# Opening stage of a two-layer encoder trunk: where the position-bias lines, the modulation sums and the first weight split stand

## The chip, the cores and the metric

The kernel runs on one core of one Trainium2 chip. The metric is the device time of one execution in microseconds (us); lower is better. Five engines work side by side, each through its own list of instructions in order: TensorE (PE, matrix products, with PEld for its weight loads), VectorE (DVE), ScalarE (ACT), GpSimd (POOL) and SyncE (SP, which here only issues transfers). The profile also records the TensorE clock that was granted, as a share of full speed.

## The reference

Two layers act on x of 1024 tokens by 1024 features. Each layer first modulates its input with a vector computed from a condition c, then mixes tokens, then normalises:

```python
mod = jax.nn.silu(c) @ ada_w[i] + ada_b[i]
shift, scale, gate = jnp.split(mod[:, None, :], 3, axis=-1)
u = x * (1 + scale) + shift
y = mixer_dilated(u, a_w_in[j], a_w_out[j], rel_bias)      # layer 0
x = layernorm(DEEPNORM_ALPHA * x + gate * y, ln_g[i], ln_b[i])
```

Layer 0 projects u with `a_w_in` to q, k, v and a gate (1152 columns each) and runs windowed attention in 18 heads of three groups with dilations 1, 4 and 16. The logits get a bias that depends only on the distance between key and query: a row of a 32-row table per bucket of distance and head. Layer 1 is a latent attention; the change does not touch it. All data are float32.

## The kernel before, in words

A float32 product is made of three faster ones. Each operand is split into a rounded "high" part (`uh`, `wh`) and the rest (`ul`, `wl`); the product is wh.uh + wl.uh + wh.ul, summed in PSUM (`mm3`, L90). The split of a 128x1024 weight tile (`w_split`, L102) is one ScalarE pass for the high part and one subtraction, on VectorE in the opening, for the low part.

Features lie on partitions. The 1024 features of u are eight **channel blocks** dd = 0 to 7 of 128 features by 1024 tokens. The opening (`startup`, L156) forms u block by block as its data land, and projects it at once to the q, k and v columns of head pair 0: three weight blocks b = 0, 1, 2, each two PSUM banks of 512 tokens. A channel block gives each weight block six 512-column products (`in_block`, L254): three parts by two halves, so 18 in all and 144 for the opening. When they end, `layer_a_attention` (L657) begins the projections of the next pair (L92 to L94).

For each channel block, the shift and the scale of its 128 features are needed as a column, 256 sums over 1024 values of silu(c). The weights `ada` for that come in two tiles of 128 x 1024, one MB together; they hold eight chunks k of 256 columns. `mod_acc` (L206) adds up SHARE[dd] of the chunks on VectorE into one tile, each term a 128x256 instruction. `mod_sums` (L218) sums over partitions on TensorE: one matmul of one column for each chunk left and one for the VectorE tile, for shift and for scale. The profile shows each such float32 matmul as two rows. `mod_col` (L229) adds the bias column `bcol` on ScalarE, `u_hi` (L236) makes uh (and u itself, which replaces x in `xc`) on ScalarE, `u_lo` (L247) makes ul on VectorE.

While the first data travel, TensorE multiplies zeros (`zeros`, L163; ZEROS = (10, 6) gives the ten at the start and the six after the first sums, and one stands after every second matmul of the first sums).

The **position-bias lines** are one line of 512 values for each head: a 33-row one-hot table (`onehot`, 198 KB) multiplied with the bias table `rel_bias`, one matmul for each head group (`bias_line`, L336, L341 in the profile, two rows each), copied by ScalarE (L343), and written to DRAM (`bias_write`), from where `bias_tile` (L349) loads shifted copies. Before the change the tables are loaded on SP at channel block 2, line 0 is computed after block 5, and lines 1 and 2 stand at the head of `layer_a_attention`, which in the trace places them ahead of the last channel block.

In the opening every engine keeps the order in which the code is written (`manual_schedule`). In the layers behind it only TensorE and SP do; the order on ScalarE, VectorE and GpSimd is chosen there by a planner when the kernel is built. Loads of the opening go on SP's queue in written order; c and the bias columns go on ScalarE's. Large tiles come from a pool G of 33 buffers; PSUM has eight banks, six of which hold the accumulating products. `weave` (L49) interleaves lists of matmuls by their progress against a given total.

In step dd of the loop, the sums of block dd are done in one piece, then its column and u are made while the products of block dd - 1 run.

Of the kernel before, what the change touches and what calls it, by code (L numbers as in the profile page):

```python
# [15 lines left out]
F32 = mybir.dt.float32  # L16
F32R = mybir.dt.float32r
AF = mybir.ActivationFunctionType
# [51 lines left out]
class Trunk:  # L70
# [85 lines left out]
    def startup(self):  # L156
# [6 lines left out]
        def zeros(n):  # L163
            for _ in range(n):
                nc.tensor.matmul(pz, zt[:, 0:P], zt[:, P : P + 512], start=True, stop=True)

        zeros(ZEROS[0])
# [3 lines left out]
        nc.scalar.activation(self.sc, self.sc, AF.Silu)  # L171
        self.rb = KP.tile([33, P], F32, name="rb")
        nc.gpsimd.memset(self.rb, NEG)
        raws = {}
        adas, xcs = {}, {}

        def load_ada(dd):
            t = [self.gt(F32, "ada") for _ in range(2)]
            for j in range(2):
                sync.dma_start(t[j], A["ada_ss0"][dd, :, j * 1024 : (j + 1) * 1024])  # L180
            return t

        def load_x(dd):
            t = self.gt(F32, "xc")
            sync.dma_start(t, A["xt"][dd])
            return t

        def load_d(dd):
            adas[dd], xcs[dd] = load_ada(dd), load_x(dd)
# [6 lines left out]
        raws[2] = self.w_load(A["wa"][2])  # L196
# [6 lines left out]
        acc_psum = [[self.bank("ip") for _ in range(2)] for _ in range(3)]  # L203
        accs, pms = {}, {}

        def mod_acc(dd):  # L206
            w = [adas[dd][k // 4][:, (k % 4) * 256 : (k % 4) * 256 + 256] for k in range(8)]
            n = SHARE[dd]
            parts = [(w[k], self.sc[:, k : k + 1]) for k in range(8 - n)]
            if n:  # L210
                a = KP.tile([P, 256], F32, tag="ot", bufs=3, name=self.nm("acc"))
                nc.vector.tensor_scalar(a, w[8 - n], self.sc[:, 8 - n : 9 - n], None, op0=ALU.mult)
                for k in range(9 - n, 8):
                    nc.vector.scalar_tensor_tensor(a, w[k], self.sc[:, k : k + 1], a, op0=ALU.mult, op1=ALU.add)
                parts.append((a, self.ones))
            accs[dd] = parts

        def mod_sums(dd):  # L218

            parts = accs.pop(dd)  # L220
            pm = pms[dd] = self.bank("pm")
            for j in range(2):
                for i, (w, x) in enumerate(parts):
                    nc.tensor.matmul(
                        pm[:, j : j + 1], w[:, j * P : j * P + P], x, start=i == 0, stop=i == len(parts) - 1
                    )
                    yield 1.0

# [21 lines left out]
        def all_of(gen):  # L250
            for _ in gen:
                pass

        def in_block(dd, blocks=(0, 1, 2)):  # L254
            for b in blocks:
                h, l = whl[b]
                ks = slice(dd * P, dd * P + P)
                hh, hl, lh = (h, self.uh[dd]), (h, self.ul[dd]), (l, self.uh[dd])
                if dd or b:
                    todo = [(x, hf) for x in (hh, lh, hl) for hf in range(2)]  # L260
                else:
                    todo = [(hh, 0), (hl, 0), (hh, 1), (lh, 0), (lh, 1), (hl, 1)]
                seen = set()
                for n, ((w, u), hf) in enumerate(todo):
                    nc.tensor.matmul(  # L265
                        acc_psum[b][hf], w[:, ks], u[:, hf * 512 : hf * 512 + 512],
                        start=dd == 0 and hf not in seen, stop=dd == NK - 1 and n >= 4,
                    )
                    seen.add(hf)
                    yield 1.0  # L270
# [12 lines left out]
        u_lo(0, HALVES[0])  # L283
        split(0)
        u_hi(0, HALVES[1])
        u_lo(0, HALVES[1])
        all_of(in_block(0, (0,)))
        split(1)
        mod_acc(1)
        weave((in_block(0, (1,)), 6.0), (mod_sums(1), 12.0))  # L290
        split(2)
        for dd in range(1, NK):
            if dd + 2 < NK:
                load_d(dd + 2)
            if dd == 2:
                self.bias_load()
            if dd == NK - 2:
                self.a_prefetch(3)
            if dd > 1:
                all_of(mod_sums(dd))  # L300
# [5 lines left out]
            if dd == 4:  # L306
                self.bias_split()
            all_of(in_block(dd - 1, (2,) if dd == 1 else (0, 1, 2)))
            if dd == 6:
                self.bias_line(0)  # L310
        self.bias_write(0)
        all_of(in_block(NK - 1))
# [8 lines left out]
    def bias_load(self):  # L321


        nc, A = self.nc, self.A
        rb = self.rb
        rr = rb[0:32, 0:96].rearrange("a (g h) -> a g h", g=3)[:, :, 0:6]
        nc.sync.dma_start(rr, A["rel_bias"].rearrange("a (g h) -> a g h", g=3))
        oh = self.KP.tile([33, 3 * 512], F32, tag="vt", bufs=1, name="oh")
        nc.sync.dma_start(oh, A["onehot"])
        self.bias_in = rb, oh  # L330

    def bias_split(self):
# [3 lines left out]
    def bias_line(self, g):  # L336

        nc = self.nc
        rb, oh = self.bias_in
        pl = self.bank("pl")  # L340
        nc.tensor.matmul(pl, rb, oh[:, g * 512 : g * 512 + 512], start=True, stop=True)  # L341
        rows = slice(32 * g, 32 * g + 6)
        nc.scalar.copy(self.lines[rows, :], pl[rows, :])  # L343

    def bias_write(self, g):

        (self.nc.scalar if g else self.nc.sync).dma_start(self.lines_d[g], self.lines[32 * g : 32 * g + 6, :])

    def bias_tile(self, head):  # L349

# [306 lines left out]
    def layer_a_attention(self):  # L657
        nc = self.nc
        self.o = {}
        for g in (1, 2):  # L660
            self.bias_line(g)
            self.bias_write(g)
# [972 lines left out]
```

## Time and profile before

| what | value |
|---|---|
| median of 3 runs | 1371.58 us (1369.65 to 1376.36) |
| the profiled execution's own time | 1375.63 us |
| its span, first to last instruction | 1373.5 us |
| mean granted TensorE clock | 0.987 |
| TensorE busy | 1343.2 us, 98% of the span |
| VectorE, ScalarE, GpSimd busy | 853.9, 799.9, 561.0 us |
| bytes moved by DMA | 114.28 MB, of which 16.50 MB before 70 us |

How to read it: "busy" is the time in which at least one instruction of that engine is open; matmuls overlap, so a busy TensorE is not one at its peak. Lines such as L265 are lines of the kernel before. In the chain of waits, each piece is followed by the piece that it released. In the tables of stretches, a row gives the busy time and count of instructions in that stretch, and the clock granted in it.

### The profile page before, as it was taken

What the parts mean: (1) busy time and instruction counts of PE and PEld (TensorE: products, weight loads), DVE (VectorE), ACT (ScalarE), POOL (GpSimd) and SP (SyncE); (2) the same over time, 40 slices, a digit from 0 to 9 for tenths busy, and PEclk for the clock granted to TensorE, in tenths of its full rate; (3) what the DMA queues carried; (4) which work ended last, traced back from release to release, by engine and by line L of the source; (5) the groups of instructions that cost most, each with busy time, mean ns of one, the idle gap of its engine ahead of it and who ended that gap; (6) DMA issues with size and microseconds to landing.
All of it is one profiled execution on the core that took longest, in us unless ns stands there. A gap on an engine that the chain in (4) does not pass through costs nothing.

```text
span 1373.5 us, 20501 instructions
## 1 busy us (share of the span) xinstructions
PE 1343.2 (98%) x7464; PEld 1152.1 (84%) x7464; DVE 853.9 (62%) x1469; ACT 799.9 (58%) x1631; POOL 561.0 (41%) x550
## 2 busy tenths in 40 slices
PE   8999999999999999999999999999999999999996
PEld 7788888888888888888988888898889889888785
DVE  5554354445445445567734278887887888777697
ACT  3575556454443432355632288788788878887421
POOL 0142333123222366524633344735554473444573
PEclk6999999999999999999999999999999999999998
DMA  9422221113245265462154011011111111012332
GB/s 365 106 64 39 58 62 40 45 41 109 74 142 155 67 164 143 165 204 102 47 159 136 0 34 30 24 41 24 30 36 44 30 25 28 24 55 89 127 107 92
DMA packets 44980, 114.28 MB, mean 83 GB/s; under 512 B 6917, under 2 KB 13333, under 8 KB 44880
## 3 DMA queue, kind: packets, MB, share of 16 engines
q1 hardware_dynamic: 40328, 100.69, 24.0%
q0 software_dynamic: 4096, 12.24, 3.5%
q8 instruction: 59, 0.97, 0.3%
q14 instruction: 41, 0.34, 0.1%
q10 hardware_dynamic: 456, 0.05, 0.0%
HBM read 96.42 MB, written 8.67 MB: 77 GB/s over the span
## 4 chain that ended last, share of the span: by engine, by line
PE 76%; DVE 10%; ACT 7%; DMA 3%; issue 3%; POOL 0%; SPq 0%; DVEq 0%; ACTq 0%; POOLq 0%
PE pj L92 8%; PE pj L94 8%; PE pj L93 8%; PE o L1388 6%; PE t L1368 5%; PE s L92 3%; PE ip L265 3%; PE s L94 3%; PE s L93 3%; PE po L94 3%; PE po L93 3%; PE po L92 3%; PE pg L92 2%; PE pg L93 2%; PE pg L94 2%
## 5 line engine op out<-in xcount | busy, mean ns | idle before, releaser
L92 PE MATMUL pj<-uh,wh 128*128 128x512 f32 x528 | 217.2, 411 | 0.0
L94 PE MATMUL pj<-uh,wl 128*128 128x512 f32 x528 | 207.0, 392 | 0.0
L93 PE MATMUL pj<-ul,wh 128*128 128x512 f32 x528 | 206.7, 392 | 0.0
L1328 DVE TENSOR_REDUCE mb<-s 128x1 f32<-128x1024 f32 x128 | 155.8, 1218 | 49.3 <-PE s L94 48.2
L1372 DVE TENSOR_TENSOR ptl<-t,pth 128x512 fp32r<-128x512 f32 x256 | 165.3, 682 | 5.6 <-ACT pth L1371 3.5
L1371 ACT CAST pth<-t 128x512 fp32r<-128x512 f32 x256 | 139.5, 590 | 38.5 <-PE t L1368 34.5
L105 POOL TENSOR_TENSOR wl<-wraw,wh 128x1024 fp32r<-128x1024 f32 x42 | 106.2, 2535 | 121.2 <-ACT wh L104 93.1
L1336 ACT ACTIVATE pr<-s,mb 128x1024 f32<-128x1024 f32 x128 | 144.3, 1127 | 14.7 <-DVE mb L1328 14.3
L1368 PEld LDWEIGHTS t<-ident,pr 128*128 128x128 f32 x1024 | 119.3, 140 | 19.2 <-DVE ptl L1372 2.6
L1368 PE MATMUL t<-ident,pr 128*128 128x128 f32 x1024 | 133.1, 273 | 1.9 <-DVE ptl L1372 1.9
L1388 PE MATMUL o<-pth,vq 128*128 128x256 f32 x512 | 130.0, 292 | 1.5 <-DVE ptl L1372 1.5
L1388 PE MATMUL o<-ptl,vq 128*128 128x256 f32 x512 | 125.0, 282 | 0.3
L553 ACT ACTIVATE sb<-sb,stat 128x256 f32<-128x256 f32 (+1 forms) x144 | 67.1, 467 | 95.3 <-DVE stat L547 95.2
L94 PEld LDWEIGHTS pj<-uh,wl 128*128 128x128 f32 x528 | 99.1, 188 | 22.1
L1399 POOL TENSOR_TENSOR osum<-osum 64x256 f32<-64x256 f32 x64 | 47.8, 746 | 167.5 <-ACT osum L1398 166.4
L93 PEld LDWEIGHTS pj<-ul,wh 128*128 128x128 f32 x528 | 99.8, 189 | 14.0
L92 PEld LDWEIGHTS pj<-uh,wh 128*128 128x128 f32 x528 | 99.8, 189 | 14.1
L92 PE MATMUL s<-kb,q 128*128 128x512 f32 x256 | 106.4, 415 | 0.1
L93 PE MATMUL s<-kb,q 128*128 128x512 f32 x256 | 101.0, 394 | 0.0
L94 PE MATMUL s<-kb,q 128*128 128x512 f32 x256 | 100.8, 394 | 0.0
L1388 PEld LDWEIGHTS o<-pth,vq 128*128 128x128 f32 x512 | 97.1, 190 | 2.0 <-DVE ptl L1372 1.9
L1388 PEld LDWEIGHTS o<-ptl,vq 128*128 128x128 f32 x512 | 97.4, 190 | 1.0 <-DVE ptl L1372 0.9
(284 smaller groups left out, 3152.4 us busy)
## 6 DMA issues: line engine op xcount, KB each, us to landing
wraw<-wa SPq DMA_DIRECT2D x36, 512.0 KB
ada<-ada_row SPq DMA_DIRECT2D x64, 256.0 KB
wraw<-wo_a SPq DMA_DIRECT2D x18, 512.0 KB
ada<-ada_ss SPq DMA_DIRECT2D x16, 512.0 KB
kb<-kb POOLq DMA_DIRECT2D x30, 256.0 KB, 4.5
f<-f_d SPq DMA_DIRECT2D x18, 256.0 KB
xc<-xt SPq DMA_DIRECT2D x8, 512.0 KB
xr<-x SPq DMA_DIRECT2D x8, 512.0 KB
```

What stands on the lines that cost most here:

```text
L92: mm(out, wh, xh, start=start, stop=False)
L93: mm(out, wh, xl, start=False, stop=False)
L94: mm(out, wl, xh, start=False, stop=stop)
L105: (lo_engine or self.nc.gpsimd).tensor_tensor(l[:, :width], raw[:, :width], f32(h[:, :width]), op=ALU.subtract)
L553: nc.scalar.activation(sb[:, a * w : a * w + w], sb[:, a * w : a * w + w], AF.Exp, bias=stat[:, 0, hh, t : t + 1], scale=-1.0, accum_out=s ...
L1328: nc.vector.tensor_reduce(m[:, 0:1], s, axis=AX.X, op=ALU.max, negate=True)
L1336: nc.scalar.activation(pr, s, AF.Exp, bias=m[:, 0:1], accum_out=dens[u // 8][:, u % 8 : u % 8 + 1])
L1368: nc.tensor.transpose(pt[:, c * P : c * P + P], pr[:, kt * P : kt * P + P], self.ident)
L1371: nc.scalar.copy(h, src)
L1372: nc.vector.tensor_tensor(l, src, f32(h), op=ALU.subtract)
L1388: nc.tensor.matmul(po[:, 0:256], v, pts[j][x][:, c * 256 : c * 256 + 256], start=n == 0, stop=n == 15)
L1399: nc.gpsimd.tensor_tensor(w3[mine, 0:256], w3[mine, 256:512], w3[mine, 0:256], op=ALU.add)
```

## The change

Three things move in the opening, and a few queues with them.

- The tables for the bias lines are loaded first of all, on GpSimd's queue. Line 0 is computed after the ten zeros and ahead of two more; line 1 after the first sums; line 2 in the middle of the sums of channel block 1. The three lines are written to DRAM on GpSimd's queue ahead of the loop.
- The sums of channel block dd + 1 are woven into the products of channel block dd. Products follow u of their own block in the same step (before, of the block ahead). In blocks 1 to 6 the products with uh of all three weight blocks come first and those with ul last. SHARE becomes (6, 4, 4, 7, ...): VectorE adds the first SHARE[dd] chunks, and TensorE takes the rest and the VectorE tile last, shift and scale in turn.
- The first weight tile is loaded ahead of x and split ahead of the first column. The second half of the first modulation weights goes on ScalarE's queue. VectorE adds the first sums before it touches the bias column. The first zeros fall from 10 + 5 + 6 to 10 + 2 + 2.

```diff
-SHARE = (4, 3, 5, 7, 7, 7, 7, 7)
+SHARE = (6, 4, 4, 7, 7, 7, 7, 7)
-ZEROS = (10, 6)
+ZEROS = (10, 2)
...
+        self.rb = KP.tile([33, P], F32, name="rb")
+        nc.gpsimd.memset(self.rb, NEG)
+        self.bias_load()
...
         nc.scalar.dma_start(self.sc, A["c"])
+        adas[0] = load_ada(0, (sync, nc.scalar))
         nc.scalar.dma_start(self.bcol, A["ada_b0"])
...
-        load_d(0)
         raws[0] = self.w_load(A["wa"][0])
+        xcs[0] = load_x(0, HALVES)
+        raws[1] = self.w_load(A["wa"][1])
         adas[1] = load_ada(1)
-        raws[1] = self.w_load(A["wa"][1])
+        raws[2] = self.w_load(A["wa"][2])
         xcs[1] = load_x(1)
...
             pm = pms[dd] = self.bank("pm")
-            for j in range(2):
-                for i, (w, x) in enumerate(parts):
+            for i, (w, x) in enumerate(parts):
+                for j in range(2):
...
+                todo += [(b, n, w, u, hf) for n, ((w, u), hf) in enumerate(order)]
+            if 0 < dd < NK - 1:
+                todo.sort(key=lambda t: t[1] >= 4)
...
+        zeros(ZEROS[0])
+        mod_acc(0)
         nc.vector.tensor_scalar(self.bcol[:, :, 1], self.bcol[:, :, 1], 1.0, None, op0=ALU.add)
-        mod_acc(0)
+        self.bias_line(0)
+        zeros(ZEROS[1])
         for n, _ in enumerate(mod_sums(0)):
-            if n % 2:
+            if n in (1, 3):
                 zeros(1)
-        zeros(ZEROS[1])
+        self.bias_line(1, copy=False)
+        split(0)
         mod_col(0)
...
-        split(0)
...
+        self.bias_copy(1)
         mod_acc(1)
-        weave((in_block(0, (1,)), 6.0), (mod_sums(1), 12.0))
+        sums = mod_sums(1)
+        weave((in_block(0, (1,)), 6.0), (steps(sums, 6), 6.0))
+        self.bias_line(2, copy=False)
+        all_of(sums)
         split(2)
+        self.bias_copy(2)
+        for g in range(3):
+            self.bias_write(g)
         for dd in range(1, NK):
...
-            all_of(in_block(dd - 1, (2,) if dd == 1 else (0, 1, 2)))
...
+            if dd == 1:
+                all_of(in_block(0, (2,)))
+            if dd + 1 < NK:
+                weave((in_block(dd), 18.0), (mod_sums(dd + 1), 4.0 * (9 - SHARE[dd + 1])))
+            else:
+                all_of(in_block(dd))
```

More of the change, by code (lines that the diff above doesn't have):

```diff
@@ L165, in zeros, with load_ada, load_x, load_d @@
                 nc.tensor.matmul(pz, zt[:, 0:P], zt[:, P : P + 512], start=True, stop=True)
-        zeros(ZEROS[0])
+        self.rb = KP.tile([33, P], F32, name="rb")
+        nc.gpsimd.memset(self.rb, NEG)
+        self.bias_load()
+        raws = {}
+        adas, xcs = {}, {}
+        def load_ada(dd, queues=(sync, sync)):
+            t = [self.gt(F32, "ada") for _ in range(2)]
+            for j in range(2):
+                queues[j].dma_start(t[j], A["ada_ss0"][dd, :, j * 1024 : (j + 1) * 1024])
+            return t
+        def load_x(dd, parts=(slice(0, 1024),)):
+            t = self.gt(F32, "xc")
+            for sl in parts:
+                sync.dma_start(t[:, sl], A["xt"][dd][:, sl])
+            return t
+        def load_d(dd):
+            adas[dd], xcs[dd] = load_ada(dd), load_x(dd)
         nc.scalar.dma_start(self.sc, A["c"])
+        adas[0] = load_ada(0, (sync, nc.scalar))
         nc.scalar.dma_start(self.bcol, A["ada_b0"])
@@ L202, in startup @@
         self.uh, self.ul = [None] * NK, [None] * NK
[L203 removed]
+        acc_psum = [None] * 3
         accs, pms = {}, {}
@@ L208, in mod_acc @@
             n = SHARE[dd]
[L209 to L216, printed above, removed]
+            a = KP.tile([P, 256], F32, tag="ot", bufs=3, name=self.nm("acc"))
+            nc.vector.tensor_scalar(a, w[0], self.sc[:, 0:1], None, op0=ALU.mult)
+            for k in range(1, n):
+                nc.vector.scalar_tensor_tensor(a, w[k], self.sc[:, k : k + 1], a, op0=ALU.mult, op1=ALU.add)
+            accs[dd] = [(w[k], self.sc[:, k : k + 1]) for k in range(n, 8)] + [(a, self.ones)]
         def mod_sums(dd):
@@ L221, in mod_sums @@
             pm = pms[dd] = self.bank("pm")
-            for j in range(2):
-                for i, (w, x) in enumerate(parts):
+            for i, (w, x) in enumerate(parts):
+                for j in range(2):
                     nc.tensor.matmul(
-                        pm[:, j : j + 1], w[:, j * P : j * P + P], x, start=i == 0, stop=i == len(parts) - 1
+                        pm[:, j : j + 1], w[:, j * P : j * P + P], x, start=i == j == 0, stop=i == len(parts) - 1,
+                        skip_group_check=True,
                     )
@@ L254, in in_block @@
         def in_block(dd, blocks=(0, 1, 2)):
+            ks = slice(dd * P, dd * P + P)
+            todo = []
             for b in blocks:
                 h, l = whl[b]
-                ks = slice(dd * P, dd * P + P)
                 hh, hl, lh = (h, self.uh[dd]), (h, self.ul[dd]), (l, self.uh[dd])
-                if dd or b:
-                    todo = [(x, hf) for x in (hh, lh, hl) for hf in range(2)]
-                else:
[L262 to L270, printed above, removed]
+                if dd == 0 and b == 0:
+                    order = [(hh, 0), (lh, 0), (hh, 1), (lh, 1), (hl, 0), (hl, 1)]
+                elif dd == 0:
+                    order = [(x, hf) for x in (hh, hl, lh) for hf in range(2)]
+                else:
+                    order = [(x, hf) for x in (hh, lh, hl) for hf in range(2)]
+                todo += [(b, n, w, u, hf) for n, ((w, u), hf) in enumerate(order)]
+            if 0 < dd < NK - 1:
+                todo.sort(key=lambda t: t[1] >= 4)
+            for b, n, w, u, hf in todo:
+                if acc_psum[b] is None:
+                    acc_psum[b] = [self.bank("ip") for _ in range(2)]
+                nc.tensor.matmul(
+                    acc_psum[b][hf], w[:, ks], u[:, hf * 512 : hf * 512 + 512],
+                    start=dd == 0 and n in (0, 1 if b else 2), stop=dd == NK - 1 and n >= 4,
+                )
+                yield 1.0
         def split(b):
             whl.append(self.w_split(raws[b], lo_engine=nc.vector))
+        zeros(ZEROS[0])
+        mod_acc(0)
         nc.vector.tensor_scalar(self.bcol[:, :, 1], self.bcol[:, :, 1], 1.0, None, op0=ALU.add)
-        mod_acc(0)
+        self.bias_line(0)
+        zeros(ZEROS[1])
         for n, _ in enumerate(mod_sums(0)):
-            if n % 2:
+            if n in (1, 3):
                 zeros(1)
-        zeros(ZEROS[1])
+        self.bias_line(1, copy=False)
+        split(0)
         mod_col(0)
```

48 lines of the change are left out of this document (11 added, 37 removed).

## The prediction

> **What bounds the kernel now.** I read the page first, then the chain of waits of the first 90 us, then the busy time of three lines window by window, then single tiles.
>
> ```profile
> span 1373.5 us, 20501 instructions
> PE 1343.2 (98%) x7464; PEld 1152.1 (84%) x7464; DVE 853.9 (62%) x1469; ACT 799.9 (58%) x1631; POOL 561.0 (41%) x550
> PEclk6999999999999999999999999999999999999998
> ```
>
> TensorE is busy for 98% of the span, so whatever the opening loses is lost at the end. Only the first slice of 34 us shows a clock well below full. The change touches that slice and the next one.
>
> The chain of waits (start, length, what) gives the landmarks; L165 is the zero products, L224 the modulation sums, L265 the opening's projection, L341 the position-bias lines.
>
> ```profile
> 1.18 5.82 DMA bcol<-ada_b
> 7.11 0.36 DVE acc L212
> 10.16 0.64 PE pz L165
> 10.79 0.64 PE pm L224 x4
> 12.72 3.20 PE pz L165 x7
> 15.91 2.72 PE ip L265 x7
> 18.64 0.34 PE pm L224 x4
> 18.97 0.34 PE ip L265
> 23.30 2.77 PE ip L265 x6
> 26.07 3.20 PE pm L224 x16
> 29.28 7.05 PE ip L265 x18
> 36.33 0.79 PE pm L224 x8
> 37.11 4.25 PE ip L265 x18
> 56.46 1.05 PE pl L341 x2
> 57.51 0.98 PE pm L224 x8
> 62.73 1.91 PE pl L341 x4
> 64.64 4.30 PE ip L265 x18
> ```
>
> First column's sums ready at 12.72, first real product at 15.91, block 0 done at 18.64, block 1 with the second sums at 23.30, channel block 1 at 36.33, all of the opening at 64.64 + 4.30 = 68.94. After 15.91 the chain is TensorE alone. A 512-column product takes 4.25 / 18 = 0.236 us late and about 0.43 us early (2.77 / 6 = 0.46 at the edges); one row of a sum 0.79 / 8 = 0.10 late and 3.20 / 16 = 0.20 early. The early price is the clock's.
>
> Busy time per stretch (stretch, length, PE busy with the count of instructions, PEld busy, granted clock, DMA share, GB/s): zero products, then L265, then L341.
>
> ```profile
> 1.10:4.51 3.41, 2.93 (x7) 2.35 (x8) 1.00 0.74 197
> 4.51:7.93 3.42, 1.94 (x6) 0.85 (x5) 1.00 1.01 390
> 11.34:14.75 3.41, 2.90 (x6) 2.08 (x7) 0.50 1.03 418
> 14.75:18.17 3.42, 1.16 (x3) 0.34 (x2) 0.50 1.02 410
> ```
> ```profile
> 14.75:18.17 3.42, 2.46 (x6) 2.12 (x7) 0.50 1.02 410
> 18.17:21.58 3.41, 2.37 (x6) 0.80 (x5) 1.00 1.04 404
> 28.41:31.82 3.41, 2.68 (x6) 2.20 (x7) 0.50 1.04 412
> 31.82:35.23 3.41, 3.41 (x9) 2.64 (x8) 0.50 1.02 406
> 35.23:38.65 3.42, 2.77 (x12) 1.99 (x11) 1.00 1.03 410
> ```
> ```profile
> 55.71:59.13 3.42, 1.12 (x2) 0.29 (x2) 1.00 0.01 3
> 62.54:65.95 3.41, 1.98 (x4) 0.67 (x4) 1.00 0.98 106
> ```
>
> The clock moves only at these edges, 3.41 us apart, and each move answers the window before it. Counting products alone: the window full of them (31.82) is followed by 1.00, and so are the one with 9, some cut by its edges (14.75), and the first, with 2.93 of 3.41 (86%). 2.68 of 3.41 (79%) left the clock down. With the clock up, 12 products (at most 12 x 0.236 = 2.8, 83%) kept it; 6 products among 19 sum rows (6 x 0.236, 41%) lost it at 21.58 although TensorE had no gap. So sum rows hardly count. Bias lines do: the last two stretches keep 1.00 with 1.1 to 1.6 us of products, and the line rows bring them to 66% or more. Rising thus needs 79 to 86%, staying 41 to 66%.
>
> **The change part by part.**
>
> *Column 0.* The order on VectorE lets the sums of channel block 0 start when the silu ends instead of after the bias column, 5.48 against 7.11.
>
> ```profile
> 5.27 0.21 ACT L171 ACTIVATE sc<-sc 128x8 f32<-128x8 f32 x1 [1.85 <-DMA sc<-c]
> L214 DVE SCALAR_TENSOR_TENSOR acc<-ada,sc,acc 128x256 f32<-128x256 f32 x39 | 18.9, 485 | 1.4
> ```
>
> VectorE now takes six terms: 0.36 + 5 x 0.49 = 2.8, done at 8.3. The second half of the first modulation weights moves to ScalarE's queue, behind the 4 KB that landed at 5.27 and beside 512 KB more on SP; at the 390 to 418 GB/s shown, 1.05 + 0.52 MB from 1.8 us on takes till 6 to 7.5. Terms 4 and 5 then end at 8.3 to 8.6. The bias column waits behind that half; 1.18 + 5.82 plus the 1.3 us of 512 KB is 8.3, not late.
>
> TensorE must first run bias line 0, and so waits for the one-hot table, now on POOL's software queue behind a small transfer. No row shows that queue in the opening. The nearest is:
>
> ```profile
> L1219 POOL DMA_DIRECT2D kb<-kb x30: 544/552/583, 703.3 to 1177.7; - x30
> DMA to landing us min/median/max: 3.0/4.5/6.7
> ```
>
> Issue ends at about 1.0 + 2 x 0.55 = 2.1, so landing lies between 5.1 and 8.8; I take the median, 6.6, since the small table on ScalarE's queue also took 4.5 (0.72 to 5.27). Queued behind the line are two zeros, the column's sums and everything else on TensorE. Line 0: 1.05, to 7.65. Window 4.51-7.93 then has 4 products, the line and one zero, about 68%; but the sums' rows thin the next one, and I price them cold from 7.93: two zeros to 8.6, then three groups of four rows and two zeros, 5 x 0.64 = 3.2, to 11.8 (warm 2.0, to 10.6). Before: 12.72.
>
> In sentences of its own: the Trainium skill, DMA: Bandwidth & Descriptors, section Anatomy of one DMA, gives 2.0 us plus bytes / 436e3 on this queue. That would be an estimated 2.5 us for 198 KB, a landing before the ten zeros end at 5.5, and a column 1.1 us sooner than I sum it. No run here shows it in a full opening; the rows under load are longer.
>
> *First products.*
>
> ```profile
> 12.76 0.41 ACT L232 ACTIVATE mcol<-pm,bcol 128x1 f32<-128x1 f32 x2 [7.28 <-PE pm L224]
> 13.20 0.81 ACT L241 ACTIVATE uh<-xc,mcol 128x512 fp32r<-128x512 f32 x1
> L104 ACT ACTIVATE wh<-wraw 128x1024 fp32r<-128x1024 f32 x4 | 4.1, 1042 | 0.0
> L241 ACT ACTIVATE uh<-xc,mcol 128x1024 fp32r<-128x1024 f32 x7 | 8.7, 1246 | 0.2
> L248 DVE TENSOR_TENSOR ul<-xc,uh 128x1024 fp32r<-128x1024 f32 x7 | 8.6, 1226 | 13.7 <-ACT xc L243 13.7
> ```
>
> Column on ScalarE 0.41, half of uh 0.81: 13.1. The weight split runs ahead of the column in ScalarE's order; its 1.04 us (8.0 to 9.3 with line 0's copy) hides under the sums unless the weights land after 10. Line 1 stands between sums and first product; the cold price isn't shown, between 1.05 and twice that, 1.9 taken: 11.8 to 13.7. First product 13.7 against 15.91; the four fewer zeros are paid for by the line. Line 1 and two and a half products fill 11.8 to 14.75, 86% of that window, so the clock rises at 14.75. Block 0 ends about 15.7, set by VectorE's second ul half, against 18.64.
>
> *Block 1, line 2, sums 1.* Six products with twelve rows, warm: 6 x 0.236 + 12 x 0.11 = 2.7, to 18.4 (0.11 from the 0.34 + 0.34 pair, less a product, over four rows). The window 14.75-18.17 holds some 9 products, 61%, in the unknown band. Likeliest it falls: line 2 1.9, eight rows 1.6, to 21.9. Before 23.30.
>
> *Block 2, channel block 1, sums 2.* 24 x 0.43 + 20 x 0.20 = 14.3 cold, to 36.2. Sums 2 has five parts instead of four (four rows more) and is spread, so products stand alone only from 21.9 + 2.6 + 9 x 0.43 + 20 x 0.20 = 32.4. Window 31.82-35.23 reaches about 92% and lifts the clock at 35.23 as before; end 35.75, against 36.33.
>
> *The rest.* Before: products 5 x 4.25 + 4.30, sums 4 x 0.79 + 0.98, lines 1.05 + 1.91. After: the lines' 2.96 are gone, the five sums cost 8 x 0.11 each when spread, 4.4 instead of 4.14. 32.6 becomes 29.95. Block dd now follows its own u directly; its first 12 products need uh alone, and sums end after 7 of 18 products, leaving 11 x 0.236 = 2.6 us for 0.41 + 1.25 of ScalarE. VectorE's 0.35 + 6 x 0.49 + 1.23 = 4.5 per block stays under 5.1. With no cover each block would lose up to 1 us.
>
> SP is freed of the wait for line 0; the copies and the three writes lie on ScalarE and POOL, idle there. The planner orders the other engines of the later layers anew; nothing prices that, taken as 0, within 2 us either way.
>
> Sum: 35.75 + 29.95 = 65.7 against 68.94, **3.2 us less**. The span of 1373.5 becomes 1370.3, the profiled 1375.63 becomes 1372.4. The runs' median is 1371.58, so I forecast 1368.4.
>
> **Rivals.**
> *The clock holds.* If 55 to 60% of a window keeps it up, it stays from 14.75 on: line 2 to 19.4, sums 20.3, uh of block 1 at 22.0, channel block 1 in 18 x 0.236 + 20 x 0.11 = 6.5, to 28.5. That is 7.8 sooner, with the 2.7 of the rest 10.5: 1361.1. For it: 66% kept it. Against: 41% did not, and spreading the sums puts several windows at 50 to 61%. The Trainium skill, TensorE: Matmul & The Clock Gate, Part 1, ties the fall to a whole idle window; by that rule nothing here would fall, and this rival is the outcome. The trace disagrees at 21.58, where a busy TensorE lost its clock.
>
> *The lines come late.* The table lands at 8.8: line 0 cold to 10.7, zeros 11.55, sums 14.75, line 1 16.65, block 0 18.8 (rise at 18.17), block 1 21.5, line 2 and sums 25.0, channel block 1 39.0. 2.7 later than before, eaten by the 2.7 of the rest: no change, 1371.6. For it: 4 KB took 4.5 us at the same time. Against: the queue's median.
>
> *The thinned blocks lose the clock.* Spread over the first seven products of channel blocks 2 to 6, the sums leave a window at worst near 70%. If staying needs more than that, each block falls once; a cold window costs half of 3.41, five times 1.7 = 8.5, less 3.2: 5.3 slower, 1376.9. Against: 66% held, though with lines in it, whose weight is inferred.
>
> **Chances.** Forecast 0.42, clock holds 0.30, lines late 0.18, blocks thinned 0.10. 0.5%, 6.9 us, is about what a measurement of this kernel can tell from no change. Holding (10.5) passes it except where it holds for only some windows: faster 0.27. Five cold windows alone stay below it; more of them would not: slower 0.05. The rest, 0.68, is the same. Range: 1360.0, below holding by a share of the 2 us of the planner, to 1376.0, short of the thinned blocks and above late lines.
>
> **What would show it.** Line 0 starting at 6.6; first column near 11.8; first L265 product near 13.7; a granted clock of 1.00 in some window from 14.75 and again from 35.23 at the latest; no L341 after 25; the first projection of the attention near 65.6. A first product after 16, or 0.50 after 38.7, makes the prediction wrong upward; a clock that stays at 1.00 after 14.75, downward.

## The result and the profile after

The changed kernel took 1379.99 us, the median of 9 runs (1375.05 to 1382.30), beside 1370.35 us of the kernel before (9 runs, 1366.42 to 1376.36): the ratio is 1.0051, with a 95% interval of 1.0031 to 1.0070. Measured once more beside the experiments, it took 1376.83 us (7 runs) against 1370.66 us (31 runs), 1.0042 [1.0024, 1.0060]. So the change costs about 0.4 to 0.5%: the forecast of 1368.4 us had the wrong sign, its range ended too low at 1376.0, and slower by over 0.5% had been given a chance of 0.05.

The profiled execution of the changed kernel took 1375.97 us. The head of its page:

```profile
span 1374.2 us, 20481 instructions
PE 1340.5 (98%) x7449; PEld 1148.2 (84%) x7449; DVE 855.9 (62%) x1471; ACT 799.2 (58%) x1631; POOL 566.6 (41%) x555
PEclk9999999999999999999999999999999999999998
```

TensorE's busy time and the other engines' are nearly those of before (1343.2 and 853.9, 799.9, 561.0). The clock row seems to say that the opening ran at full clock. It did not: this trace holds no change of the clock before 34.55, and what lies ahead of the first change is shown as 1.00. The chain of waits (start, length, what; L164 zero products, L222 sums, L274 products, L352 bias lines) gives the landmarks, and the spacing of the products gives the clock:

```profile
1.06 0.56 POOL zqr L514 x2
1.68 0.56 POOL zqr L514 x2
2.23 0.69 POOL rb L340
2.92 7.18 DMA oh<-onehot
10.24 2.04 PE pl L352 x2
12.28 1.15 PE pz L164 x2
13.43 0.64 PE pm L222 x4
...
16.63 2.00 PE pl L352 x2
18.63 3.28 PE ip L274 x7
...
26.40 2.00 PE pl L352 x2
28.40 1.80 PE pm L222 x8
30.20 3.20 PE ip L274 x7
...
37.97 2.40 PE ip L274 x10
```

Seven products take 3.28 and 3.20 us, 0.46 each, and a line of two instructions 2.04 to 2.00: that is the price of the low clock, and it is paid up to 34.55. The column is ready at 16.63 (12.72 before), the first real product starts at 18.63 (15.91 before).

In the trace of the second measurement the clock is recorded from the start of the opening. Busy time per stretch: first two stretches over all engines (stretch, length, busy time and count of PE, PEld, DVE, ACT and POOL, granted clock, DMA share, GB/s), then PE and PEld of the products L274 alone, then of the lines L352 alone:

```profile
15.61:19.03 3.42, 3.42 (x7) 1.80 (x8) 1.46 (x3) 2.75 (x5) 0.00 (x0) 0.50 1.03 410
22.44:25.85 3.41, 3.41 (x20) 2.48 (x20) 3.28 (x6) 0.38 (x1) 0.00 (x0) 1.00 1.03 411
```
```profile
15.61:19.03 3.42, 0.90 (x2) 0.80 (x3) 0.50 1.03 410
19.03:22.44 3.41, 3.25 (x8) 1.73 (x7) 0.50 1.04 402
22.44:25.85 3.41, 1.82 (x4) 0.73 (x4) 1.00 1.03 411
25.85:29.26 3.41, 2.60 (x6) 2.19 (x7) 0.50 1.03 408
```
```profile
15.61:19.03 3.42, 2.07 (x2) 0.49 (x2) 0.50 1.03 410
22.44:25.85 3.41, 1.12 (x2) 0.29 (x2) 1.00 1.03 411
```

The stretch from 15.61 holds one line and two products, and with the last sums ahead of them TensorE has no gap in it (PE busy 3.42 of 3.42); it is followed by 0.50. The next, with eight products, lifts the clock at 22.44, when block 0 is through and block 1 has begun. The stretch that then runs at full clock holds four products between sum rows and line 2, and it loses the clock again at 25.85, until 39.50.

### The profile page after: what moved, and what is told of

Its sections match the earlier page's. It is cut to its first block, busy times and chain, and to the rows that moved or that the text cites. A ratio compares the mean times of both kernels' runs of the same rounds, so it can differ in the third digit from the quotient of the medians.

```text
span 1374.2 us, 20481 instructions
## 1 busy us (share of the span) xinstructions
PE 1340.5 (98%) x7449; PEld 1148.2 (84%) x7449; DVE 855.9 (62%) x1471; ACT 799.2 (58%) x1631; POOL 566.6 (41%) x555
## 4 chain that ended last, share of the span: by engine, by line
PE 77%; DVE 9%; ACT 7%; issue 3%; DMA 3%; SPq 0%; POOL 0%; DVEq 0%; ACTq 0%; POOLq 0%
PE pj L91 8%; PE pj L93 8%; PE pj L92 8%; PE o L1400 6%; PE t L1380 5%; PE s L91 3%; PE s L92 3%; PE s L93 3%; PE ip L274 3%; PE po L93 3%; PE po L91 3%; PE po L92 3%; PE pg L91 2%; PE pg L93 2%; PE pg L92 2%
## 5 line engine op out<-in xcount | busy, mean ns | idle before, releaser
L104 POOL TENSOR_TENSOR wl<-wraw,wh 128x1024 fp32r<-128x1024 f32 x42 | 106.6, 2542 | 90.3 <-ACT wh L103 65.1
L1380 PEld LDWEIGHTS t<-ident,pr 128*128 128x128 f32 x1024 | 119.3, 140 | 19.2 <-DVE ptl L1384 2.6
```

The lines of the kernel that those rows point to most:

```text
L104: (lo_engine or self.nc.gpsimd).tensor_tensor(l[:, :width], raw[:, :width], f32(h[:, :width]), op=ALU.subtract)
L1380: nc.tensor.transpose(pt[:, c * P : c * P + P], pr[:, kt * P : kt * P + P], self.ident)
```

## The experiments

Four theories. **Theory 1**: the one-hot table on GpSimd's queue lands late and holds TensorE. **Theory 2**: the loss lies behind the opening, in the planner's order of later layers. **Theory 3**: the sums spread between the products of channel block 1 thin its stretches, so the clock rises later. **Theory 4**: the six zero products between the first sums and the first real product, which the change dropped for a bias line, had helped to lift the clock, and a line of 33 rows does not do their work.

The twelve kernels, in us. Each stands beside runs of the kernel before on the same chip (e1 to e4: median 1371.11, clock 0.9913; z1, z2, c1 and c2: 1371.78, 0.9913; z3, b1, c3 and after_again: 1370.66, 0.9916). The changed kernel itself ran beside z3, b1 and c3 only, so e1 to e4, z1 and c1 are set against it by their ratios. "Clock" is the mean granted clock of all runs of a kernel; it is told too high where the first rise is missing in a record, as in four of e4's runs (0.995 to 0.997 at 1376.3 to 1378.9 us).

| kernel | edit | median | ratio [95%] | clock |
|---|---|---|---|---|
| e1_tables_hw | changed; tables on the SP and ScalarE queues | 1372.08 | 1.0012 [0.9993, 1.0032] | 0.9906 |
| e2_sums2_piece | changed; sums of block 2 in one piece | 1373.76 | 1.0019 [1.0001, 1.0037] | 0.9896 |
| e3_lines_late | changed; lines and tables where they were | 1377.47 | 1.0059 [1.0034, 1.0083] | 0.9864 |
| e4_tables_sums2 | e1 and e2 together | 1375.62 | 1.0024 [1.0004, 1.0044] | 0.9917 |
| z1_six_zeros | changed; six zero products behind line 1 | 1372.64 | 1.0015 [0.9997, 1.0034] | 0.9913 |
| z2_before_no_six | before; without its six | 1376.05 | 1.0020 [1.0000, 1.0040] | 0.9885 |
| z3_zeros_33rows | before; its six on 33 partitions | 1374.73 | 1.0023 [1.0006, 1.0040] | 0.9883 |
| b1_line0_early | before; line 0 early, tables on GpSimd's queue | 1374.12 | 1.0030 [1.0014, 1.0045] | 0.9919 |
| c2_before_share | before; VectorE takes more of the early sums | 1372.67 | 1.0008 [0.9993, 1.0024] | 0.9911 |
| c1_zeros_lines_mid | changed; six zeros, lines after blocks 3 to 5, first weights all on SP's queue | 1366.96 | 0.9970 [0.9954, 0.9986] | 0.9942 |
| c3_sums2_piece | c1 with e2's edit | 1367.60 | 0.9981 [0.9966, 0.9995] | 0.9941 |
| after_again | the changed kernel | 1376.83 | 1.0042 [1.0024, 1.0060] | 0.9877 |

**e1_tables_hw** (theory 1).

```
-        self.bias_load()
...
         nc.scalar.dma_start(self.sc, A["c"])
+        self.bias_load()
...
-        nc.gpsimd.dma_start(rr, A["rel_bias"].rearrange("a (g h) -> a g h", g=3))
+        nc.scalar.dma_start(rr, A["rel_bias"].rearrange("a (g h) -> a g h", g=3))
-        nc.gpsimd.dma_start(oh, A["onehot"])
+        nc.sync.dma_start(oh, A["onehot"])
```

> The changed kernel, with the two tables of the bias lines loaded on the hardware queues: the one-hot table first on SP, the small table on ScalarE's queue behind c. Nothing is left out. Theory 1, the late table: the changed kernel loses because TensorE stands behind the one-hot table, which lands at 10.2 on GpSimd's queue. Then line 0 starts by 6 us instead of 10.24, the first column's sums end near 12 instead of 16.6, and the time falls by 3 to 5 us below the changed kernel's 1380. Theory 2, behind the opening: the loss comes from the planner's new order of the later layers, and the opening hides the wait. Then the time stays within 2 us of the changed kernel's.

Its timeline (start, length, engine, line, operation, and in brackets the idle time ahead and what ended it):

```profile
7.35 1.09 PE L352 MATMUL pl<-oh,rb 33*128 33x512 f32 x2 [1.14 <-DMA rb<-rel_bias]
10.50 1.01 DVE L213 SCALAR_TENSOR_TENSOR acc<-ada,sc,acc 128x256 f32<-128x256 f32 x2 [1.63 <-DMA ada<-ada_ss]
14.12 0.41 ACT L231 ACTIVATE mcol<-pm,bcol 128x1 f32<-128x1 f32 x2 [4.04 <-PE pm L222]
```

Line 0 starts 2.9 us sooner than in the changed kernel (10.24) and the column comes at 14.12 instead of 16.67, two us later than expected. The ratio is 1.0012 against the changed kernel's 1.0042 and 1.0051, so most of the loss seems gone, as theory 1 has it; but its interval overlaps that of 1.0042, and e4, which holds the same edit, shows less of it (1.0024). Part of the 2.9 us is the earlier issue: the one-hot table is issued at 0.73 instead of 2.92, rel_bias at 1.16 instead of 2.17, and it is the 2.2 KB of rel_bias that line 0 now waits for. The rest of the delay has only changed its owner: the second half of the modulation weights now lands at 10.50.

**e2_sums2_piece** and **e4_tables_sums2** (theory 3).

```
-            if dd + 1 < NK:
+            if dd == 1:
+                all_of(mod_sums(2))
+                all_of(in_block(1))
+            elif dd + 1 < NK:
```

> The changed kernel, with the sums of channel block 2 in one piece ahead of the products of channel block 1, as before the change; the tables stay on GpSimd's queue. Theory 3, the thinned block: with these sums woven in, products stand close only for 3.1 us ahead of the weave, and the clock's rise near 34.6 is missed in about half of the executions and then comes some 10 us later, worth 5 us. Then the times here no longer split into 1375 to 1377 and 1380 to 1382, the median falls by 2 to 4 us, and the trace shows the rise within one window of 3.4 us after the pieces end. Theories 1 and 2: no change within 2 us, the spread stays.

> Both edits at once: tables on the hardware queues, and the sums of channel block 2 in one piece. Theories 1 and 3 together: 6 to 9 us below the changed kernel, 1368 to 1373, level with the kernel before or a little below it, with a narrower spread. Theory 2: within 2 us of the changed kernel's 1380.

Alone the edit lowers the ratio from the changed kernel's 1.0042 to 1.0019, as theory 3 has it; on top of e1's it raises the median by 3.5 us, on the same chip. In both comparisons the intervals overlap. In the two profiles the lasting rise comes at 39.17 and 38.48, no sooner than without (34.55 and 39.50 in the two of the changed kernel, 37.55 in e1). Two signs for one edit speak against theory 3 but do not settle it; c3 below tries it once more.

**e3_lines_late** (theories 1 and 4 against 2).

```
-        self.bias_line(0)
...
-        self.bias_line(1, copy=False)
...
+            if dd == 5:
+                self.bias_line(0)
+            if dd == 6:
+                self.bias_write(0)
```

> The changed kernel, with the bias lines and their tables where and on the queues they were before the change (line 0 after channel block 5, lines 1 and 2 at the head of the attention); all else as changed. Theory 1: the wait for the table and the lines' 4 to 6 us in the cold opening go, 3 us come back late: 4 to 6 us below the changed kernel, near 1375, and the first product starts near 12 to 14. Theory 2: as the planner's input is then as before, the time falls to 1370 with the opening's end unchanged. Theory 3 alone: the split of the times stays.

The first product starts at 13.10, sooner than in the kernel before, and yet the clock is low from 8.27 to 35.58. So a column that comes in time is not enough once the zero products are gone. The median of 1377.47 says less, for this kernel brought a wait of its own. Its chain, and two of its stretches over all engines (PE, PEld, DVE, ACT, POOL, clock):

```profile
56.93 1.07 PE pl L350 x2
...
58.02 0.05 ACT lines L356
...
58.50 0.40 ACT mcol L230 x2
...
58.92 1.25 ACT uh L239
...
60.22 0.80 PE ip L273
```
```profile
56.06:59.47 3.41, 1.92 (x6) 0.67 (x4) 0.83 (x2) 1.42 (x4) 0.00 (x0) 1.00 0.01 2
59.47:62.88 3.41, 2.67 (x8) 2.35 (x9) 1.23 (x1) 1.94 (x2) 0.00 (x0) 0.50 0.37 56
```

The copy of line 0 stands on ScalarE ahead of column 6, TensorE is idle for 2.2 us (58.0 to 60.2), and the clock, gone at 59.47, stays low until 66.3. Some of its 6 us are this wait.

**z1_six_zeros**, **z2_before_no_six** and **z3_zeros_33rows** (theory 4, from both kernels).

```
         self.bias_line(1, copy=False)
+        zeros(6)
```
```
-ZEROS = (10, 6)
+ZEROS = (10, 0)
```
```
-        zeros(ZEROS[1])
+        for _ in range(ZEROS[1]):
+            nc.tensor.matmul(pz, zt[0:33, 0:P], zt[0:33, P : P + 512], start=True, stop=True)
```

> The changed kernel with six more zero products behind bias line 1, right ahead of the first real product; nothing else is changed, nothing left out. Theory 4, the clock is not woken: what is lost is mainly granted clock, because the six zeros that ran on into the first products are gone and line 1 does not count as activity. Then 2.6 us of useless work lower the median by 2 to 5 us below the changed kernel's 1380, and the mean granted clock of the executions rises (the changed kernel's lie at 0.983 to 0.988 where an early rise is recorded). Theory 1, the late table alone: the zeros only delay, 1381 to 1383.

> The kernel before, without the six zeros behind the first sums (ZEROS = (10, 0)). Theory 4: the clock rises later in most executions, 3 to 6 us slower than before, 1374 to 1377, and the granted clocks move from 0.987 to 0.994 down by 0.003 or so. Theory 1, in which only waits and work on the path count: the first product starts up to 0.9 us sooner (weights ready at 15.0 instead of 15.9), 1369.5 to 1371.

> The kernel before with its six late zero products on 33 partitions in place of 128; nothing else moves. If only occupied time on TensorE raises the clock, this is the kernel before: median within 1 us of it, mean granted clock about .991. If products of 33 rows count for little or nothing (as the bias lines of the changed kernel suggest, which filled 17.49 to 20.90 without a rise), it behaves like the kernel without the six: median 3 to 5 us above the kernel before, mean clock about .988.

Put back into the changed kernel, the six delay the first product by another 2.2 us, to 20.78 (18.56 in the first trace of the changed kernel, in the same view), and still the ratio falls from 1.0042 to 1.0015; the two intervals overlap. Taken from the kernel before, their absence costs 4.3 us in the median and 3.1 in the mean of the runs, with an interval that begins at no change (1.0000 to 1.0040). On 33 partitions they are as good as absent: median +4.1, mean +2.8, clock 0.9883 against 0.9885 without any.

z3's trace shows why, over all engines (PE, PEld, DVE, ACT, POOL, clock), and in the last row for the zeros of 33 rows alone:

```profile
13.00:16.41 3.41, 3.41 (x8) 2.26 (x9) 2.80 (x4) 3.41 (x5) 0.00 (x0) 0.50 1.03 417
16.41:19.82 3.41, 3.41 (x12) 2.83 (x11) 3.31 (x7) 0.68 (x1) 0.00 (x0) 0.50 1.04 402
19.82:23.23 3.41, 3.41 (x26) 3.19 (x26) 3.12 (x6) 0.00 (x0) 0.00 (x0) 1.00 1.03 412
```
```profile
13.00:16.41 3.41, 2.73 (x6) 1.61 (x6) 0.50 1.03 417
```

The stretch from 13.00 holds nothing but the six zeros and the first products, without a gap, and 0.50 follows; the next holds eight products of 128 rows and sum rows, and 1.00 follows. Since the zero products of 33 rows take TensorE's time as the full ones do (2.86 us for six, in z3 and in z1), occupied time alone is not what the clock answers to.

In z1's trace, the products L274 alone:

```profile
18.65:22.06 3.41, 1.28 (x3) 1.32 (x4) 0.50 1.02 396
22.06:25.47 3.41, 3.37 (x10) 1.53 (x8) 1.00 1.04 414
25.47:28.89 3.42, 1.45 (x6) 1.05 (x6) 1.00 1.02 407
28.89:32.30 3.41, 2.94 (x7) 1.15 (x7) 1.00 1.04 415
```

With the six zeros ahead of three products the clock rises at 22.06, where block 0 has begun 1.3 us earlier instead of 4.3; ten products fall into the stretch that follows, and the clock is not lost again.

The other traces sort the same way. In the six of kernels with six full zeros at this place (before, z1, b1, c1, c2, c3) the clock is up at most 3.3 us after the first real product starts (b1's by the spacing of its products). In the eight without (both of the changed kernel, e1 to e4, z2, z3) it comes 3.9 to 4.5 us after it in five, and over 15 us after it in three (e3, e4, the first of the changed kernel). So the six are no condition of a rise: z2's own trace, of an execution of 1369.96 us, rises at 19.2, loses the clock at 22.6 and has it again from 26.0. An explanation that fits, and is argued: ahead of the first sum rows the kernel before has 5.9 us of unbroken 128-row products (12.72 to 18.64) and the changed one 3.28, and a stretch is 3.41 long, so the long run fills most of one wherever the edges fall, and the short one only by luck.

**b1_line0_early** (theory 1 without theory 4: the six zeros stay).

```
+        self.bias_load()
+        self.bias_split()
...
+        self.bias_line(0)
         nc.vector.tensor_scalar(self.bcol[:, :, 1], self.bcol[:, :, 1], 1.0, None, op0=ALU.add)
...
-            if dd == 6:
-                self.bias_line(0)
...
-        nc.sync.dma_start(oh, A["onehot"])
+        nc.gpsimd.dma_start(oh, A["onehot"])
```

> The kernel before with line 0 and its two tables moved to the start of the opening (tables on GpSimd's queue, lines 1 and 2 stay where they are), with its six zero products kept. Theory 1 (the line delays the column of row block 0): column 3 to 4 us later than 12.76, and the median 1 to 3 us above the kernel before (what the column loses, less the 1 us that the late line 0 cost). Theory 4 (the zero products decide by the clock): six zeros still stand at the column, so the clock still rises in the opening in most executions and the median is within 1 us of the kernel before.

```profile
2.95 6.58 DMA oh<-onehot
...
9.66 2.04 PE pl L338 x2
```
```profile
17.80 0.41 ACT L234 ACTIVATE mcol<-pm,bcol 128x1 f32<-128x1 f32 x2 [5.49 <-PE pm L226]
```

The table takes 6.58 us from its issue, line 0 starts at 9.66, the column comes 5.0 us after that of the kernel before (12.76). The median rises by 3.5 us, more than theory 1 had it, and theory 4's "within 1 us" is missed. The clock does rise with the zeros: the second product starts 0.36 us and the third 0.23 us after the one before it. So the late line costs time with the zeros in place, too.

**c2_before_share**.

```
-SHARE = (4, 3, 5, 7, 7, 7, 7, 7)
+SHARE = (4, 6, 7, 7, 7, 7, 7, 7)
```

> The kernel before with SHARE = (4, 6, 7, 7, ...): VectorE takes more of the sums of channel blocks 1 and 2, so TensorE has 12 and 8 rows instead of 24 and 16 between the products. Theories 3 and 4: the stretches in which the clock falls get shorter, more executions keep it from 18 us on, 2 to 4 us under the kernel before, 1367 to 1369. If only work on the path counts: sums 1 wait for VectorE (about 1.5 us more there), 24 to 32 cold rows less are worth 2 to 3 us, so within 1 us of before.

No gain, where theories 3 and 4 had 2 to 4 us. In its profile the opening ends at 65.1, 3.8 us sooner than in the profile of before, but the attention gives nearly all of it back, with the clock low from 427.1 to 430.5; what makes it do so was not followed up.

**c1_zeros_lines_mid** and **c3_sums2_piece**: the six zeros in, the lines moved behind the early blocks, and theory 3 again.

```
-        adas[0] = load_ada(0, (sync, nc.scalar))
+        adas[0] = load_ada(0)
...
-        self.bias_line(0)
-        zeros(ZEROS[1])
...
-        self.bias_line(1, copy=False)
+        zeros(6)
...
+            if dd in (4, 5, 6):
+                self.bias_copy(dd - 4)
+                self.bias_write(dd - 4)
...
+            if dd in (3, 4, 5):
+                self.bias_line(dd - 3, copy=False)
```

> The changed kernel with both halves of the first modulation weights on SP, six zeros in the place of line 1, and the three lines after channel blocks 3, 4 and 5 with their copies behind the next uh; sums spread as in the change. First column near 10, first product near 12 to 13. Theory 4: woken ahead of the products, it ends level with the kernel before or under it, 1365 to 1371. Theory 3, that the thin weave itself loses the clock whatever stands ahead of it: it falls again in block 1 and the rise comes after 30, 1372 to 1376.

> The variant that keeps six zeros and puts the bias lines behind blocks 3, 4 and 5, now with the sums of block 2 in one piece behind row block 1's column instead of spread between block 1's products. Theory 3 (the thinned block 1 costs the clock): the median falls 1 us or more below that variant's 1366.97, or its spread narrows. Otherwise: within 1 us of it, and 3 to 5 us below the kernel before.

c1's chain, and its stretches with the products L274 alone:

```profile
8.48 0.98 PE pm L222 x4
9.46 2.77 PE pz L164 x6
12.23 2.99 PE ip L274 x7
...
38.12 1.05 PE pl L350 x2
```
```profile
11.88:15.29 3.41, 3.19 (x7) 2.10 (x8) 0.50 1.03 408
15.29:18.70 3.41, 2.53 (x6) 1.20 (x7) 1.00 1.03 411
18.70:22.11 3.41, 2.90 (x8) 1.78 (x7) 0.50 1.04 402
22.11:25.53 3.42, 3.42 (x8) 1.50 (x8) 1.00 1.03 408
```

The first product starts at 12.23, the clock rises at 15.29, falls once and is up from 22.11 to the end of the opening, at 62.3 against 68.9 before. This kernel beats both others: 1366.96 us, 4.8 below the kernel before on the same chip, which is itself below the changed one. Since it moves the lines and brings back the zeros at once, it does not tell the two apart. Its traced execution is its slowest (1371.05): of the 6.7 us that its opening gains on the trace of before, 2.4 are given back behind it, with the clock low from 459.1 to 462.5; the cause is open. Block 2's sums in one piece (c3) give 1367.60, within 0.7 us, with the same clock: with the zeros in place, theory 3 finds nothing. For the changed kernel itself, without them, e2 and e4 leave it open.

**after_again**.

> The changed kernel itself, on the chip of the three others. All theories: 1376 to 1382, some 6 to 10 us above the kernel before. Theory 4: mean granted clock .985 to .988 against about .991 before, and no rise of the clock between the first products and the end of block 1 in its trace, or a rise that is lost before 15 us.

The median and the mean clock (0.9877) came as expected. Theory 4's sign in the trace did not: between the first products and the end of block 1 the clock rises, at 22.44, and is lost at 25.85. Its trace is the second one read in the section on the result.

## Why the prediction was wrong

**Which step failed.** "Sum rows hardly count. Bias lines do", and from it "Line 1 and two and a half products fill 11.8 to 14.75, 86% of that window, so the clock rises at 14.75". The second measurement has nearly this stretch, 15.61 to 19.03: one line, two products, the last of the sums, no gap, and no rise. The trace of before had shown lines only in stretches that kept a clock already up, and in the same stretches stood products; I read the lines' share as activity because the sum needed it. z3 tests the inference with nothing else moved: 33 rows instead of 128, a stretch filled with them without a rise, and the six zeros lose their worth.

With this falls a price: "the four fewer zeros are paid for by the line". I took them for filling that costs TensorE's time and brings nothing. Six of them take 2.86 us (z1's chain has 18.13 to 20.99, z3's on 33 partitions as long). z2 prices them at some 3 us of the kernel's time (mean 3.1, interval 0 to 5.5), z3 at 2.8. I should have read the row 14.75:18.17 of before, which ends at a rise and holds three zero products, as theirs.

**The mis-sized term** beside it is the table: landing 6.6, bounds 5.1 to 8.8. Measured, it landed at 10.10 and 9.67 and line 0 started at 10.24 and 9.80, outside both bounds. The chain shows why: the fills of zqr stand on GpSimd ahead of the two issues, as they do in the trace of before (L499, 1.06 to 2.23), so the second issue begins at 2.92 and ends at 3.5, where I had 2.1. The row that I used counts from the start of an issue (in the same view the one-hot table's landing is 7.2, 2.92 to 10.10); I added it to the end. So the landing took 7.18 and 6.75 us, above that row's maximum (6.7) and far from its median (4.5). The Trainium skill, DMA: Bandwidth & Descriptors, section Anatomy of one DMA, would have put an estimated 2.5 us; the trace disagrees.

Sizes: the table makes 3.6 of the 4.9 us by which the first product came late. From there to the end of block 1 the clock adds most: 30.2 instead of 21.9, 8.3 late. The forecast counted on the one stretch of full clock from 14.75, worth half of 3.41 us; the first trace has none before 34.55, and the second one loses the one that it gets. The experiments put the two about on a level: with the tables sooner (e1) or with the zeros back (z1), the ratio is 1.0012 and 1.0015.

By the other steps, in their order:

- *Sums of VectorE* "end at 8.3 to 8.6": they ended at 10.29, since the second half of the weights on ScalarE's queue landed at 9.28:

```profile
9.28 1.01 DVE L213 SCALAR_TENSOR_TENSOR acc<-ada,sc,acc 128x256 f32<-128x256 f32 x2 [1.37 <-DMA ada<-ada_ss]
10.24 2.04 PE L352 MATMUL pl<-oh,rb 33*128 33x512 f32 x2 [4.02 <-DMA oh<-onehot]
```

  The line hid this delay; in e1, with the line early, it sets the column.
- *Line 0 to the column*, 4.15 us: 12.28 to 16.63, 4.35. Line 0 itself at the low clock, 2.04 instead of 1.05. Column to first product, 1.9: 2.00. So the first product's 18.63 instead of 13.7 is 3.6 of the table, 1.0 of line 0's clock and 0.3 of the rest; "a first product after 16" was the sign that I had named for an error upward.
- *Block 1 with line 2 and its sums*, 6.2 with the products at full clock: 8.9 all at half, from 21.3 to 30.2.
- *The rise at 35.23 as before*: 34.55 in the first trace, 39.50 in the second. *Channel block 1* ended at 40.0 and 40.5, not at 35.75.
- *The rest*, 29.95: 40.0 to 70.4 by the starts of the products that follow, 30.4. The blocks held 5.03 us apiece, so the rival of the thinned blocks did not come about, and the lines' 2.96 us are gone as forecast. The half microsecond more is a wait that I had not seen, ahead of the opening's last products:

```profile
64.44 1.13 issue
65.56 1.05 ACT wh L103
66.66 0.50 PE pj L91
67.39 3.19 PE ip L274 x14
```

  Two projections of the attention run between 66.66 and 67.39, while the last block's products with ul wait for VectorE.
- *Planner, 0 within 2 us*: from the end of the opening in the chain, 70.6 instead of 68.9, to the end of the span, 1374.2 instead of 1373.5, the two profiles differ by 1.0 us, and the second trace of the changed kernel by 0.6. Theory 2 finds no room there.

Of the **rivals**, "the lines come late" named the right place and half the mechanism. It priced a table at 8.8 with the clock rising at 18.17 all the same, put the end of channel block 1 at 39.0 (measured 40.0 and 40.5), and so came out at no change.

**Where the time is.** In most of these kernels the time of a run follows its granted clock. On the chip of after_again the kernel before runs from 1366.8 us at 0.994 to 1375.2 at 0.988; a straight line through its 31 runs gives 1.2 us for each 0.001, and 0.001 of the span is 1.37. Taking (1 - clock) x 1374 us from each run leaves a mean of 1359.0 us for the kernel before and 1358.6 for the changed one: the work is worth the same. The clocks, 0.9916 and 0.9877, differ by 0.0039, or 5.4 us, and the means, 1370.5 and 1375.5, by 5.0. So the lines' gain late and the column's loss early seem to cancel, and the clock makes the difference, in the opening by the traces. c1 stands at 1359.5 and 0.9942. The split is good to a few us only: it puts z3 at 1357.2 and z1 at 1362.0. (Where the first rise is missing in the records, as in b1's and e4's profiles, the clock is told too high and this split does not hold.)

That is also why the profile was the wrong base. I carried the gap between the profiled 1375.63 and the median of 1371.58 over as a constant. It was the draw of the clock in one execution (0.987), the very thing that the change acts on. Of the two profiles, 0.3 us apart, the one shows the kernel before near its slowest and the other the changed kernel near its fastest. Of the 11.6 us between forecast and median, 3.6 lie between the trace that was forecast (1372.4) and the one that came (1375.97); the other 8 are these two draws, 4 each.

**What stays open.** What loses the clock: six products in a stretch lost it before at 21.58 and kept it in z1 at 28.89, so neither my band of 41 to 66% nor the count alone decides. And four of z1's twelve runs took 1377.0 to 1378.5 us at the clock of the other eight (1370.8 to 1373.6); no trace of one of the four was taken. Nor does a trace show the kernel before in one of its faster executions; that its clock then rises early and stays rests on its mean clock, 0.991 to 0.994 against the trace's 0.987.

## What to carry to other kernels

Before dropping filler products ahead of a wait, read what the clock does in the stretch that holds them, and price them by a run without them: here six products on zeros took 2.9 us of TensorE, and without them the kernel was some 3 us slower in the mean (interval 0 to 5.5). Useful work put in their place did not do what they did while it was of 33 rows instead of 128. And what goes ahead of the first real product should not hang on a transfer that shares the crowded opening; with the lines after blocks 3 to 5 and the six zeros kept, c1 was 0.30% [0.14, 0.46] faster than the kernel before.

## What was unexpected of the hardware

- A stretch of 3.41 us without a gap on TensorE did not raise the clock where 33-row products made most of it (PE busy 3.42 of 3.42 from 15.61, next stretch 0.50), while eight products of 128 rows in 3.41 us did. z3's trace agrees (33-row zeros for 2.73 of 3.41 us from 13.00, next stretch 0.50), and so do its 11 runs: mean clock 0.9883, against 0.9916 with 128 rows.
- The full clock was lost at 25.85 after a stretch in which TensorE was never idle. The Trainium skill, TensorE: Matmul & The Clock Gate, Part 1, ties the fall to an idle window; the trace disagrees, as it did at 21.58 in the kernel before.
- The executions of one kernel differ by 4.7 us (c2) to 16 us (e3), 8.4 in the kernel before, and the granted clock mostly goes with them (e3: 0.991 at the fastest, 0.980 at the slowest). The same part of the Trainium skill calls the window free-running, so that where the work falls in it changes from run to run, and puts the ramp under 1% of a typical span. The traces agree with the first: the lasting rises of the changed kernel's two, 34.55 and 39.50, are 4.95 us apart, which is no multiple of 3.41. Of the second, the runs show the whole time at the low clock: the mean clocks leave 0.8% of the span before and 1.2% after, and the difference is the size of what this change was about.
- Of 198 KB on GpSimd's queue in the full opening, issue to landing took 6.58 us (b1) to 7.18 us (after). The queue is not the whole of it: on ScalarE's queue the 2.2 KB of rel_bias took 5.89 us (e4, issued at 1.17), and line 0 of e1 waited for them until 7.35.
